# SBUF tiles at chosen distances from one another, one r block in the attention's PSUM banks, and the last down projection in token rows

## The chip, the cores and the metric

One core of one Trainium2 chip runs the whole program. The metric is the device time of one execution in microseconds (us), smaller is better. The kernel before takes 1268.01 us, the median of 3 runs (1267.92 to 1268.65).

## The reference

A decoder trunk of two layers over 256 tokens of width 1024, in float32. Each layer is a half-step SwiGLU (hidden width 2816), a mixer of two parallel branches (a three-branch sparse attention with 8 heads and a chunked gated linear attention, called GLA, with 4 heads), and a second half-step SwiGLU; a final RMS norm ends it.

```python
def swiglu(x, w_gate, w_up, w_down):
    return (jax.nn.silu(x @ w_gate) * (x @ w_up)) @ w_down
...
    for l in range(DEPTH):
        x = x + 0.5 * swiglu(rmsnorm(x, ffn1_norm[l]), ffn1_w_gate[l], ffn1_w_up[l], ffn1_w_down[l])
        h = rmsnorm(x, mix_norm[l])
        proj = h @ w_in[l]
        q_a, kv_a, g_a, q_b, k_b, v_b, a_lr, r_b, g_merge = jnp.split(proj, offsets, axis=-1)
...
        o_b = o_b.reshape(B, S, GLA_HEADS * GLA_DV) * jax.nn.silu(r_b)
        gm = jax.nn.sigmoid(g_merge).reshape(B, S, 2, D)
        y = gm[:, :, 0] * (o_a @ w_branch_nsa[l]) + gm[:, :, 1] * (o_b @ w_branch_gla[l])
        x = x + y @ w_out[l]
        x = x + 0.5 * swiglu(rmsnorm(x, ffn2_norm[l]), ffn2_w_gate[l], ffn2_w_up[l], ffn2_w_down[l])
    return rmsnorm(x, final_norm)
```

## The kernel before

**Numbers in two parts.** Every large product is made of three: a float32 value is kept as a rounded high part and a low part, and high times high, high times low and low times high are summed in PSUM. `mm3` writes these as three matmuls. `mm2` writes them as two: the high weight against the activation's high and low part side by side (512 passing columns), then the low weight against the high part alone (256). A matmul has a standing operand (128 x 128, loaded into TensorE by a weight load) and a passing operand (streamed through it).

**Which operand stands.** In `ffn`, `T_pair`, the `wo` products and the down projections (tiles `ff`, `mm` of 256 columns, `wo`, `dn`) the weights stand and the activations pass, so the result has features on partitions. In `block` and the merge (`mm` of 512 columns, `mg`) the activations stand and a row of 512 weights passes, so the result has tokens on partitions. The last output feature block (j = 7) of `dn` and `wo` uses `mm3` with 256 passing columns.

**Weights.** `Weights` holds one list of chunks in the order of use. SP loads a chunk into one of 3 `raw` tiles, ScalarE rounds it into `wh` (`cast`, line 76) and VectorE subtracts it into `wl` (line 86), half a chunk at a time; `prep` is called between the matmuls of the chunk ahead, and `take` hands a chunk out. Each of `wh` and `wl` has 3 tiles.

**Memory.** Tiles lie in SBUF in the order in which the pools are opened: constants (with the `xs` tiles that hold the activation's two parts), small ones, `t4` (15 tiles of 4 KB a partition: the hidden values `h`, `oa`, `ob`, `y` and more), `t2` (9 of 2 KB), `raw`, `wh` and `wl`. In the built program, taken modulo 512 bytes, the `xs` tiles start at 128, the `t4`, `t2`, `raw`, `wh` and `wl` tiles at 480. All slices that a large matmul reads start at a multiple of 512 bytes from their tile's start (but for `vg`). In this text the distance of a matmul is the start of its standing slice less the start of its passing slice, modulo 512 bytes: 352 where weights stand against `xs` (`ff`, `mm` of 256 columns), 0 where they stand against `t4` tiles (`dn`, `wo`), 160 where `xs` stands and weights pass (`mm` of 512 columns), 0 where `oa` and `ob` stand and weights pass (`mg`).

**PSUM.** Two banks have the tag `mm`, six the tag `sd`, each set used in turn. In the mixer the main stream of `block` uses the two `mm` banks: two blocks for v, two for r (the gate's input, evacuated by `r_evac`: a tanh on ScalarE, then a multiply-add on VectorE, line 541), four for the merge gates (`gm`). `slot` drives the side work (attention, then GLA) from generators between the matmuls, in the `sd` banks. A block's first matmul waits until its bank has been read out.

**The end.** After the last down projection (`next_gain is None`), `add_half` adds each feature block to x, a square on ScalarE and a sum over feature blocks give the norm, `final_x` transposes x times the final gain into token rows (tile `fin`), one matmul of ones gives each token's sum, GpSimd raises it to -1/2, and ScalarE and VectorE scale four 128 x 512 tiles, which SP writes out with four transfers.

Of the kernel before, what the change touches and what calls it, by code (L numbers as in the profile page):

```python
# [15 lines left out]
P = 128  # L16
# [19 lines left out]

class Weights:
# [10 lines left out]
    def load(self, n):  # L48
        while self.n_load < min(n, len(self.chunks)):
            ap, rows, cols = self.chunks[self.n_load]  # L50
# [11 lines left out]
    def cast(self):  # L62
# [13 lines left out]
        self.nc.scalar.activation(wh[:, s], self.raw[c][:, s], AF.Copy)  # L76
# [3 lines left out]
    def prep(self):  # L80
# [5 lines left out]
        self.nc.vector.tensor_sub(wl[:, s], self.raw[c][:, s], wh[:, s].bitcast(F32))  # L86
# [5 lines left out]
    def take(self):  # L92
        c = self.n_take
        self.n_take += 1
        while self.n_prep < (c, 1):
            self.prep()
        _, rows, cols = self.chunks[c]
        wh, wl = self.split.pop(c)
        return tuple(x[:, : rows * cols].rearrange("p (r c) -> p r c", c=cols) for x in (wh, wl))


class Trunk:
# [63 lines left out]
    def square(self, j, own=False):  # L166
# [5 lines left out]
        elif own:  # L172
            self.own = sq
        else:
            self.nc.vector.tensor_add(self.acc, self.acc, sq)
# [52 lines left out]
    def final_x(self, j):  # L228

        if j == 0:  # L230
            self.fin = [[self.bank(f"fin{t}{e}") for e in range(2)] for t in range(2)]
        xg = self.xg.pop(j)
        for tt in range(2):
            self.nc.tensor.transpose(self.fin[tt][j // 4][:, j % 4 * P : j % 4 * P + P], xg[:, tt * P : tt * P + P], self.ident)


    def ffn(self, l, f, next_gain, hook=None):
# [14 lines left out]
        def gate2(u):  # L252
            nc.vector.tensor_mul(u[:, 0:T], u[:, 0:T], self.rbc)
# [64 lines left out]
        while lows:  # L318
            low()
        for j in range(NK):  # L320
            b = self.bank(f"dn{self.uid()}", "mm")
            for half in range(2):
# [7 lines left out]
                if next_gain is None and half == 0 and j > 0:  # L330
                    self.final_x(j - 1)
                    if j == NK - 1:
                        self.st = self.bank("stl")
                        self.sums(self.acc, True, False)
            self.add_half(j, b)
            if next_gain is None:
                self.square(j, own=j == NK - 1)
                xg = self.t2(f"xg{j}")[:, 0:T]
                nc.vector.tensor_scalar(xg, self.x[j], self.final[:, j : j + 1], None, op0=OP.mult)
                self.xg[j] = xg  # L340
            else:
                self.post_x(j, next_gain[:, j : j + 1])
# [10 lines left out]
    def add_half(self, j, b):  # L353
        for s in (slice(0, T), slice(T, 2 * T))[: 2 if j < NK - 1 else 1]:
            self.nc.vector.scalar_tensor_tensor(self.x[j], b[:, s], 0.5, self.x[j], op0=OP.mult, op1=OP.add)  # L355


    def mixer(self, l, next_gain):
# [152 lines left out]
        def block(evac):  # L511

            bs = [self.bank(f"mm{self.uid()}", "mm") for _ in range(2)]
# [32 lines left out]
        for n in range(2):  # L546
            block(r_evac(n))
# [514 lines left out]
    def go(self):  # L1062
# [3 lines left out]
        with ExitStack() as st:  # L1066
# [33 lines left out]
            self.xg = {}  # L1100
            self.w1 = {}
            sm = cp.tile([P, 80], F32, name="sm")
# [217 lines left out]
```

## Time and profile before

| what | value |
|---|---|
| median of 3 runs | 1268.01 us (1267.92 to 1268.65) |
| the profiled execution: its own time, and its span | 1268.17 us, 1266.4 us |
| busy share of TensorE (PE), VectorE, ScalarE, GpSimd | 99%, 72%, 56%, 4% |
| mean granted clock of TensorE | 0.998 of full |
| moved from and to HBM | 225.12 MB, 2.63 MB; 180 GB/s over the span |

The span runs from the first to the last instruction that the trace shows; the execution's own time is 1.8 us longer. A PE row's length is a modelled pipeline time and longer than the pace: the matmuls overlap, so the pace is read from the starts of rows that follow one another.

### The profile page before, as it was taken

How to read it: one execution, taken by the hardware profiler on the slowest of the kernel's cores; microseconds unless marked ns; L12 is line 12 of the kernel's file. 1: busy time of each engine (PE TensorE's matmuls, PEld its weight loads, DVE VectorE, ACT ScalarE, POOL GpSimd, SP SyncE). 2: the span in 40 equal slices, each digit the busy share in tenths (PEclk: the TensorE clock that was granted, in tenths of full speed). 3: DMA queues.
4: the chain of work that ended last, by engine and by line, in shares of the span. 5: the costliest groups of instructions: out<-in, count | busy, mean ns of one | idle time of the engine just before them, and what ended most of it. 6: DMA issues, size and time to landing. Idle time of an engine off the chain costs nothing.

```text
span 1266.4 us, 18985 instructions
## 1 busy us (share of the span) xinstructions
PE 1251.6 (99%) x7396; PEld 1076.0 (85%) x7396; DVE 913.9 (72%) x1690; ACT 711.8 (56%) x1265; POOL 50.5 (4%) x60
## 2 busy tenths in 40 slices
PE   9999999999999999999999999999999999999997
PEld 7888889987778888888888888999777788888886
DVE  6888766774755778886578886567656668888753
ACT  5666545566644556655456664456675445566542
POOL 2001101000010000000010000010000100000000
PEclk9999999999999999999999999999999999999999
DMA  7576767334534445545665546573344354555451
GB/s 272 193 230 211 255 201 264 132 124 137 178 118 144 181 168 205 187 154 198 209 224 208 179 150 205 173 283 135 111 156 164 103 199 148 184 200 185 165 190 59
DMA packets 41001, 227.43 MB, mean 180 GB/s; under 512 B 6949, under 2 KB 8109, under 8 KB 21328
## 3 DMA queue, kind: packets, MB, share of 16 engines
q1 hardware_dynamic: 34352, 213.27, 48.7%
q0 software_dynamic: 5840, 11.87, 2.8%
q8 instruction: 58, 0.95, 0.3%
q10 hardware_dynamic: 720, 1.09, 0.3%
q14 instruction: 31, 0.25, 0.1%
HBM read 225.12 MB, written 2.63 MB: 180 GB/s over the span
## 4 chain that ended last, share of the span: by engine, by line
PE 80%; issue 15%; DVE 2%; ACT 2%; DMA 1%; POOL 0%; POOLq 0%; DVEq 0%; ACTq 0%
PE ff L129 19%; PE ff L130 10%; PE dn L129 9%; PE mm L122 7%; PE mm L123 6%; PE mm L124 6%; PE dn L130 4%; PE wo L129 2%; PE mg L122 2%; PE mg L124 2%; PE mg L123 2%; PE O L150 2%; PE o L150 1%; PE s L150 1%; PE wo L130 1%
## 5 line engine op out<-in xcount | busy, mean ns | idle before, releaser
L76 ACT ACTIVATE wh<-raw 128x1024 fp32r<-128x1024 f32 (+3 forms) x445 | 423.4, 967 | 183.6 <-issue 112.3
L86 DVE TENSOR_TENSOR wl<-raw,wh 128x1024 fp32r<-128x1024 f32 (+3 forms) x445 | 491.3, 1119 | 44.0 <-ACT wh L76 43.7
L129 PE MATMUL ff<-xs,wh 128*128 128x512 f32 x1408 | 489.9, 392 | 0.4 <-DVE xs L162 0.4
L130 PE MATMUL ff<-xs,wl 128*128 128x256 f32 x1408 | 393.9, 280 | 0.7 <-DVE wl L1144 0.5
L129 PEld LDWEIGHTS ff<-xs,wh 128*128 128x128 f32 x1408 | 264.4, 188 | 59.2 <-ACT wh L1143 0.8
L130 PEld LDWEIGHTS ff<-xs,wl 128*128 128x128 f32 x1408 | 264.3, 188 | 1.7 <-DVE wl L1144 1.1
L129 PE MATMUL dn<-h,wh 128*128 128x512 f32 x616 | 218.3, 399 | 0.0
L130 PE MATMUL dn<-h,wl 128*128 128x256 f32 x616 | 173.0, 281 | 0.0
L129 PEld LDWEIGHTS dn<-h,wh 128*128 128x128 f32 x616 | 115.7, 188 | 28.3
L139 DVE TENSOR_TENSOR u<-ff,u 128x256 f32<-128x256 f32 x176 | 74.7, 425 | 60.9 <-ACT u L138 60.9
L130 PEld LDWEIGHTS dn<-h,wl 128*128 128x128 f32 x616 | 116.4, 189 | 0.0
L122 PE MATMUL mm<-wh,xs 128*128 128x512 f32 x256 | 106.2, 415 | 2.5 <-DVE rt L541 2.5
L123 PE MATMUL mm<-wl,xs 128*128 128x512 f32 x256 | 101.5, 396 | 0.0
L124 PE MATMUL mm<-wh,xs 128*128 128x512 f32 x256 | 100.9, 394 | 0.0
L249 ACT ACTIVATE u<-u 128x256 f32<-128x256 f32 x88 | 36.8, 419 | 90.8 <-DVE u L248 90.8
L261 ACT ACTIVATE h<-u 128x256 fp32r<-128x256 f32 x88 | 36.8, 418 | 83.9 <-DVE u L260 83.9
L122 PE MATMUL mm<-xs,wh 128*128 128x256 f32 x256 | 73.8, 288 | 0.0
L124 PE MATMUL mm<-xs,wl 128*128 128x256 f32 x256 | 71.7, 280 | 0.0
L123 PE MATMUL mm<-xs,wh 128*128 128x256 f32 x256 | 71.6, 280 | 0.0
L138 ACT ACTIVATE u<-ff 128x256 f32<-128x256 f32 x176 | 65.6, 373 | 9.8 <-PE ff L130 5.4
L355 DVE SCALAR_TENSOR_TENSOR xs<-dn,xs 128x256 f32<-128x256 f32 x60 | 25.5, 424 | 56.0 <-PE dn L130 38.5
L122 PEld LDWEIGHTS mm<-wh,xs 128*128 128x128 f32 x256 | 48.1, 188 | 19.3 <-issue 4.7
(244 smaller groups left out, 1618.1 us busy)
## 6 DMA issues: line engine op xcount, KB each, us to landing
raw<-in_gu SPq DMA_DIRECT2D x85, 1024.0 KB, 4.9
raw<-in_wd SPq DMA_DIRECT2D x64, 704.0 KB, 4.1
raw<-in_wr SPq DMA_DIRECT2D x32, 1024.0 KB, 4.8
raw<-in_wt SPq DMA_DIRECT2D x16, 1024.0 KB, 5.1
raw<-in_wb SPq DMA_DIRECT2D x12, 1024.0 KB, 4.8
w<-in_w POOLq DMA_DIRECT2D x16, 512.0 KB, 8.6
raw<-in_wo SPq DMA_DIRECT2D x8, 1024.0 KB, 4.9
raw<-in_vg SPq DMA_DIRECT2D x4, 592.0 KB, 3.7
```

The source lines that it names most:

```text
L76: self.nc.scalar.activation(wh[:, s], self.raw[c][:, s], AF.Copy)
L86: self.nc.vector.tensor_sub(wl[:, s], self.raw[c][:, s], wh[:, s].bitcast(F32))
L122: mm(out, lh, rh, start=first, stop=False, skip_group_check=True)
L123: mm(out, lh, rl, start=False, stop=False, skip_group_check=True)
L124: mm(out, ll, rh, start=False, stop=last, skip_group_check=True)
L129: mm(b, lh, x[2], start=first, stop=False, skip_group_check=True)
L130: mm(b[:, 0:T], ll, x[0], start=False, stop=last, skip_group_check=True)
L138: self.nc.scalar.activation(o, b[:, T : 2 * T], AF.Copy)
L139: self.nc.vector.tensor_add(o, b[:, 0:T], o)
L150: self.nc.tensor.matmul(out, l, r, start=first, stop=last, skip_group_check=True)
L249: nc.scalar.activation(g, g, AF.Silu)
L261: nc.scalar.activation(hs[i][0], h, AF.Copy)
```

## The change

The weight tiles get 2176 columns in place of 2048, and chunks whose weights pass (`vg`, `wr`, `wb` and the new `wl`) are written 40 columns (160 bytes) into them, by the fourth entry of a chunk. Two unused tiles (`gap0`, 512 bytes, before `t4`; `gap1`, 352 bytes, before `wh`) move the pools, the `sm` tile loses 8 columns, and the memory set aside for GpSimd's transfer descriptors is halved to 8192 bytes a partition. In the built program, modulo 512 bytes, `xs` stays at 128, `t4`, `t2` and `raw` start at 128 and `wh` and `wl` at 480, so a chunk written 160 bytes on starts at 128. The distance is then 352 for every product with standing weights (`ff`, `mm` of 256 columns, `dn`, `wo`) and 0 for every one with passing weights (`mm` of 512 columns, `mg`, the new last `dn`).

The second r block takes its two banks from the `sd` set. The last down projection (`last_down`) lets weights pass and `h` stand: x enters the four token-row banks first by 16 float32 matmuls with the identity, then 11 chunks of four weight rows follow, the last three for one token half and then for the other; the factor 0.5 moves into `gate2`. The squares come from PSUM with a running sum, the gain is a row that GpSimd loads by broadcast, and each token half is written out by two transfers, on ScalarE's and SP's queues. The old path (`final_x`, the sums, four transfers at the end) is gone.

```diff
+SHIFT = 40
...
-        _, rows, cols = self.chunks[c]
+        _, rows, cols, off = self.chunks[c]
         if part == 0:
             self.split[c] = tuple(
-                self.pools["w"].tile([P, 2048], F32R, name=f"w{x}{c}", tag=f"w{x}") for x in "hl"
+                self.pools["w"].tile([P, 2176], F32R, name=f"w{x}{c}", tag=f"w{x}") for x in "hl"
             )
         wh, wl = self.split[c]
         cut = (rows + 1) // 2 * cols
         s = slice(0, cut) if part == 0 else slice(cut, rows * cols)
-        self.nc.scalar.activation(wh[:, s], self.raw[c][:, s], AF.Copy)
+        self.nc.scalar.activation(wh[:, s.start + off : s.stop + off], self.raw[c][:, s], AF.Copy)
         self.cast_done.append((c, part, s))
...
-        self.nc.vector.tensor_sub(wl[:, s], self.raw[c][:, s], wh[:, s].bitcast(F32))
+        off = self.chunks[c][3]
+        o = slice(s.start + off, s.stop + off)
+        self.nc.vector.tensor_sub(wl[:, o], self.raw[c][:, s], wh[:, o].bitcast(F32))
...
         def gate2(u):
-            nc.vector.tensor_mul(u[:, 0:T], u[:, 0:T], self.rbc)
+            if next_gain is None:
+                nc.vector.scalar_tensor_tensor(u[:, 0:T], u[:, 0:T], 0.5, self.rbc, op0=OP.mult, op1=OP.mult)
+            else:
+                nc.vector.tensor_mul(u[:, 0:T], u[:, 0:T], self.rbc)
...
         while lows:
             low()
+        if next_gain is None:
+            self.last_down(hs)
+            return
         for j in range(NK):
             b = self.bank(f"dn{self.uid()}", "mm")
             for half in range(2):
...
-                if next_gain is None and half == 0 and j > 0:
-                    self.final_x(j - 1)
-                    if j == NK - 1:
-                        self.st = self.bank("stl")
-                        self.sums(self.acc, True, False)
             self.add_half(j, b)
-            if next_gain is None:
-                self.square(j, own=j == NK - 1)
-                xg = self.t2(f"xg{j}")[:, 0:T]
-                nc.vector.tensor_scalar(xg, self.x[j], self.final[:, j : j + 1], None, op0=OP.mult)
-                self.xg[j] = xg
-            else:
-                self.post_x(j, next_gain[:, j : j + 1])
+            self.post_x(j, next_gain[:, j : j + 1])
...
+    def last_down(self, hs):
+        nc, W = self.nc, self.W
+        bs = [[self.bank(f"dn{e}{tt}", "sd" if e else "mm") for tt in range(2)] for e in range(2)]
+        pre = [self.small([P, 2], f"pre{tt}", 1) for tt in range(2)]
+        xg = [[self.t2(f"xg{e}{tt}") for tt in range(2)] for e in range(2)]
+        def residual(e):
+            for tt in range(2):
+                for q in range(4):
+                    self.mm(bs[e][tt][:, q * P : q * P + P], self.x[4 * e + q][:, tt * P : tt * P + P], self.ident, q == 0, False)
+        def products(c, tt, wh, wl):
+            for r in range(4):
+                e, k = divmod(4 * c + r, NFF)
+                s = slice(tt * P, tt * P + P)
+                self.mm3(bs[e][tt], hs[k][0][:, s], hs[k][1][:, s], wh[:, r], wl[:, r], False, k == NFF - 1)
+        def gained(e, tt):
+            sq = self.t2(f"fsq{e}{tt}")
+            nc.scalar.activation(sq, bs[e][tt], AF.Square, accum_out=pre[tt][:, e : e + 1])
+            nc.vector.tensor_mul(xg[e][tt], bs[e][tt], self.fin[:, e * 512 : e * 512 + 512])
+        def first(tt):
+            gained(0, tt)
+            nc.vector.tensor_scalar(pre[tt][:, 0:1], pre[tt][:, 0:1], 1.0 / D, EPS, op0=OP.mult, op1=OP.add)
+        def finish(tt):
+            gained(1, tt)
+            ms = self.small([P, 1], "fms")
+            nc.vector.tensor_scalar(ms, pre[tt][:, 1:2], 1.0 / D, pre[tt][:, 0:1], op0=OP.mult, op1=OP.add)
+            rs = self.small([P, 1], "frs")
+            nc.gpsimd.tensor_tensor(rs, ms, self.mhalf[:, 0:1], op=OP.pow)
+            for e in range(2):
+                o = xg[e][tt]
+                if e == 0:
+                    nc.scalar.activation(o, o, AF.Copy, scale=rs)
+                    nc.scalar.dma_start(self.out[tt, :, 0:512], o)
+                else:
+                    nc.vector.tensor_scalar(o, o, rs, None, op0=OP.mult)
+                    nc.sync.dma_start(self.out[tt, :, 512:1024], o)
+        residual(0)
+        for c in range(8):
+            if c == 5:
+                residual(1)
+            wh, wl = W.take()
+            for tt in range(2):
+                products(c, tt, wh, wl)
+                W.prep()
+            if c in (3, 4):
+                W.prep()
+            if c == 5:
+                for tt in range(2):
+                    first(tt)
+        ws = [W.take() for _ in range(3)]
+        for tt in range(2):
+            for x in range(3):
+                products(8 + x, tt, *ws[x])
+            finish(tt)
...
-        def block(evac):
-            bs = [self.bank(f"mm{self.uid()}", "mm") for _ in range(2)]
+        def block(evac, tag="mm"):
+            bs = [self.bank(f"mm{self.uid()}", tag) for _ in range(2)]
...
-            block(r_evac(n))
+            block(r_evac(n), ("mm", "sd")[n])
...
+            gap = pool("gap", 1)
+            gap.tile([P, 128], F32, name="gap0")
             self.pt4 = pool("t4", 15)
             self.pt2 = pool("t2", 9)
-            pools = dict(raw=pool("raw", N_RAW), w=pool("w", N_SPLIT))
+            pools = dict(raw=pool("raw", N_RAW))
+            pool("gap2", 1).tile([P, 88], F32, name="gap1")
+            pools["w"] = pool("w", N_SPLIT)
...
-                        chunks.append((a["gu"][l, f, i], 16, P))
+                        chunks.append((a["gu"][l, f, i], 16, P, 0))
+                    if (l, f) == (L - 1, 1):
+                        for i in range(11):
+                            chunks.append((a["wl"][i], 4, 512, SHIFT))
+                        return
                     for i in range(16):
-                        chunks.append((a["wd"][l, f, i], 11, P))
+                        chunks.append((a["wd"][2 * l + f, i], 11, P, 0))
                 ffn_chunks(0)
                 wt = [(a["wt"][l, i], 16, P) for i in range(8)]
-                vg = [(a["vg"][l, i], 4, 296) for i in range(2)]
-                chunks += wt[:1] + vg + wt[1:] + [(a["wr"][l, i], 4, 512) for i in range(16)]
-                chunks += [(a["wb"][l, i], 4, 512) for i in range(6)]
-                chunks += [(a["wo"][l, i], 16, P) for i in range(4)]
+                wide = lambda n, k, c: [(a[n][l, i], 4, c, SHIFT) for i in range(k)]
+                wt = [w + (0,) for w in wt]
+                chunks += wt[:1] + wide("vg", 2, 296) + wt[1:] + wide("wr", 16, 512) + wide("wb", 6, 512)
+                chunks += [(a["wo"][l, i], 16, P, 0) for i in range(4)]
...
+                def gain_row(i):
+                    if i == 11:
+                        self.fin = self.t4("fin")
+                        nc.gpsimd.dma_start(self.fin, a["fin"].broadcast_to([P, D]))
...
-    nc = _bacc.Bacc("TRN2", target_bir_lowering=False, num_devices=1)
+    nc = _bacc.Bacc("TRN2", target_bir_lowering=False, num_devices=1, dynamic_dma_scratch_size=8192)
```

The moves that the order of instructions shows, on the engines that wait or are waited for:

TensorE, first mixer, from the last matmuls of the second r block to the first of the merge gates (`mm` is the PSUM bank written, then passing and standing operand), before:

```order
1875 L122 MATMUL mm_3311<-wh_3250,xs_97 128x512
1876 L123 MATMUL mm_3311<-wl_3251,xs_97 128x512
1877 L124 MATMUL mm_3311<-wh_3250,xs_97 128x512
1878 L122 MATMUL mm_3406<-wh_3301,xs_90 128x512 [waits DVE_49]
1879 L123 MATMUL mm_3406<-wl_3302,xs_90 128x512
1880 L124 MATMUL mm_3406<-wh_3301,xs_90 128x512
```

The same place in the changed kernel:

```order
1875 L129 MATMUL mm_3319<-wh_3258,xs_105 128x512
1876 L130 MATMUL mm_3319<-wl_3259,xs_105 128x512
1877 L131 MATMUL mm_3319<-wh_3258,xs_105 128x512
1878 L129 MATMUL mm_3414<-wh_3309,xs_98 128x512 [waits Activation_49]
1879 L130 MATMUL mm_3414<-wl_3310,xs_98 128x512 [waits DVE_49]
1880 L131 MATMUL mm_3414<-wh_3309,xs_98 128x512
```

The first gate matmul waited for VectorE before, which is the read-out of the r block's bank; in the changed kernel it waits for ScalarE and the next for VectorE, for the two parts of its weights.

TensorE, the start of the last down projection in the changed kernel (before, `dn` matmuls with standing weights followed the `ff` matmuls directly):

```order
6601 L137 MATMUL ff_11353<-xs_105,wl_11239 128x256
6602 L157 MATMUL dn_11406<-cst,xs 128x128 [waits DMAHW0_49]
6603 L157 MATMUL dn_11406<-cst,xs 128x128 x3
6604 L157 MATMUL dn_11407<-cst,xs 128x128 x4
6605 L129 MATMUL dn_11406<-wh_11291,h_704_10293 128x512 [waits Activation_49]
6606 L130 MATMUL dn_11406<-wl_11292,h_704_10293 128x512 [waits DVE_49]
6607 L131 MATMUL dn_11406<-wh_11291,h_704_10293 128x512
```

Eight float32 matmuls of x with the identity stand ahead of the first product, and the products come in threes of 512 columns.

VectorE, the end of the program, before (`xs` is x, `st` the sums) and then changed:

```order
1671 L355 SCALAR_TENSOR_TENSOR xs<-dn_11815,xs 128x256 [waits PE_49]
1672 L355 SCALAR_TENSOR_TENSOR xs<-dn_11815,xs 128x256 [waits DVE_49]
1673 L175 TENSOR_TENSOR sq_11459<-sq_11459,sq_11873 128x256 [waits Activation_49]
1674 L339 TENSOR_SCALAR xg_11876<-xs,sm 128x256 [waits DVE_49]
1675 L355 SCALAR_TENSOR_TENSOR xs<-dn_11878,xs 128x256 [waits PE_49]
1676 L339 TENSOR_SCALAR xg_11953<-xs,sm 128x256 [waits DVE_49]
1677 L192 TENSOR_SCALAR ms_11957<-stl 128x2 [waits PE_49]
1678 L1231 TENSOR_SCALAR out_11966<-fin_11495,rs_11959 128x512 [waits PE_49,Pool_49]
1679 L1231 TENSOR_SCALAR out_11972<-fin_11497,rs_11959 128x512 [waits PE_49]
```

```order
1642 L371 TENSOR_TENSOR xg_11414<-dn_11408,fin 128x512 [waits Activation_49]
1643 L380 TENSOR_SCALAR fms_11734<-pre_776_11410 128x1 [waits DVE_49]
1644 L389 TENSOR_SCALAR xg_11414<-xg_11414,frs_11736 128x512 [waits Pool_49]
1645 L371 TENSOR_TENSOR xg_11415<-dn_11409,fin 128x512 [waits Activation_49]
1646 L380 TENSOR_SCALAR fms_11781<-pre_777_11411 128x1
1647 L389 TENSOR_SCALAR xg_11415<-xg_11415,frs_11783 128x512 [waits Pool_49]
```

The additions to x, the gained copy and the read of the sums are replaced, for each token half, by one product with the gain row, one small step and one scaling; the product waits for ScalarE, whose square reads the same bank.

## Rows read from the trace of the kernel before

**Rows 1.** The page's first part: busy us, share of the span, instructions.

```profile
PE 1251.6 (99%) x7396; PEld 1076.0 (85%) x7396; DVE 913.9 (72%) x1690; ACT 711.8 (56%) x1265; POOL 50.5 (4%) x60
```

**Rows 2.** Busy us (count) of PE, PEld, DVE, ACT, POOL, PEclk, DMA share, GB/s.

```profile
311.79:325.55 13.76, 13.76 (x61) 11.09 (x60) 9.52 (x13) 13.70 (x20) 0.00 (x0) 1.00 0.38 127
...
460.00:570.00 110.00, 110.00 (x636) 96.87 (x636) 93.67 (x165) 68.11 (x123) 0.00 (x0) 1.00 0.52 179
...
1193.50:1257.54 64.04, 64.04 (x394) 57.05 (x392) 35.79 (x60) 24.26 (x37) 0.00 (x0) 1.00 0.42 136
```

**Rows 3.** Timeline of PE in `ff`, 58 pairs apart: start, us, what.

```profile
499.81 0.39 PE L129 MATMUL ff<-xs,wh 128*128 128x512 f32 x1
...
519.91 0.39 PE L129 MATMUL ff<-xs,wh 128*128 128x512 f32 x1
```

**Rows 4.** Timeline of PE in `dn` of the first layer's second half-step, 43 pairs apart.

```profile
594.77 0.28 PE L130 MATMUL dn<-h,wl 128*128 128x256 f32 x1
...
609.96 0.28 PE L130 MATMUL dn<-h,wl 128*128 128x256 f32 x1
```

**Rows 5.** Timeline of PE, 66 matmuls of `dn` (j = 7), then 47 of `mm`.

```profile
188.61 0.28 PE L122 MATMUL dn<-h,wh 128*128 128x256 f32 x1
...
196.52 0.28 PE L122 MATMUL mm<-xs,wh 128*128 128x256 f32 x1
...
202.04 0.28 PE L124 MATMUL mm<-xs,wl 128*128 128x256 f32 x1
```

**Rows 6.** Timeline of PE in the r blocks: 59 matmuls from first to second.

```profile
311.80 0.39 PE L122 MATMUL mm<-wh,xs 128*128 128x512 f32 x1
...
325.56 0.39 PE L124 MATMUL mm<-wh,xs 128*128 128x512 f32 x1
```

**Rows 7.** Timeline of PE in the merge: 71 matmuls from first to second.

```profile
389.96 0.40 PE L122 MATMUL mg<-wh,oa 128*128 128x512 f32 x1
...
406.10 0.39 PE L124 MATMUL mg<-wh,ob 128*128 128x512 f32 x1
```

**Rows 8.** Groups by line and form on PE: count | busy us, mean ns | idle before.

```profile
L129 PE MATMUL dn<-h,wh 128*128 128x512 f32 x616 | 218.3, 399 | 0.0
L122 PE MATMUL mm<-wh,xs 128*128 128x512 f32 x256 | 106.2, 415 | 2.5 <-DVE rt L541 2.5
L129 PE MATMUL wo<-y,wh 128*128 128x512 f32 x112 | 40.5, 404 | 0.4 <-DVE y L577 0.4
```

**Rows 9.** Timeline of PE, first matmul of the merge gates, in the first mixer.

```profile
327.18 0.50 PE L122 MATMUL mm<-wh,xs 128*128 128x512 f32 x1 [1.23 <-DVE rt L541]
```

**Rows 10.** The waits of PE: who for whom, us in total, times, longest.

```profile
PE mm L122 <- DVE rt L541: 2.5, 2, 1.2
```

**Rows 11.** Timeline of VectorE around it: the second half of two weight chunks.

```profile
321.70 1.20 DVE L86 TENSOR_TENSOR wl<-raw,wh 128x1024 fp32r<-128x1024 f32 x1
...
328.33 1.22 DVE L86 TENSOR_TENSOR wl<-raw,wh 128x1024 fp32r<-128x1024 f32 x1
```

**Rows 12.** Timeline of PE: four float32 matmuls of 128 columns (eight records), and what follows.

```profile
337.30 1.05 PE L150 MATMUL ab<-qr,ga 128*128 128x128 f32 x8
338.11 0.48 PE L122 MATMUL mm<-wh,xs 128*128 128x512 f32 x1
```

**Rows 13.** Timeline of all engines from the last matmul of `dn` on.

```profile
1257.41 0.28 PE L124 MATMUL dn<-h,wl 128*128 128x256 f32 x1
1257.73 0.42 DVE L355 SCALAR_TENSOR_TENSOR xs<-dn,xs 128x256 f32<-128x256 f32 x1 [6.46 <-PE dn L124]
...
1258.72 0.61 PE L150 MATMUL stl<-ones,sq 128*128 128x1 f32 x4 [1.02 <-ACT sq L169]
...
1260.32 1.41 DVE L1231 TENSOR_SCALAR out<-fin,rs 128x512 f32<-128x512 f32 x2 [0.80 <-POOL rs L194]
1261.04 1.80 SPq L1232 DMA_DIRECT2D out<-out  x4
```

**Rows 14.** Timeline of ScalarE: the reading of a running sum after a square.

```profile
353.35 0.19 ACT L849 ACTIVATION_READ_ACCUMULATOR on<-o 128x1 f32 x1
```

More of the change, by code (lines that the diff above doesn't have):

```diff
@@ L49, in load @@
         while self.n_load < min(n, len(self.chunks)):
-            ap, rows, cols = self.chunks[self.n_load]
+            ap, rows, cols, _ = self.chunks[self.n_load]
             t = self.pools["raw"].tile([P, 2048], F32, name=f"raw{self.n_load}", tag="raw")
@@ L96, in take @@
             self.prep()
-        _, rows, cols = self.chunks[c]
+        _, rows, cols, off = self.chunks[c]
         wh, wl = self.split.pop(c)
-        return tuple(x[:, : rows * cols].rearrange("p (r c) -> p r c", c=cols) for x in (wh, wl))
+        return tuple(x[:, off : off + rows * cols].rearrange("p (r c) -> p r c", c=cols) for x in (wh, wl))
 class Trunk:
@@ L164, in split_x, with square @@
         )
-    def square(self, j, own=False):
+    def square(self, j):
         sq = self.psq.tile([P, T], F32, name=f"sq{self.uid()}", tag="sq" if j else "acc")
@@ L226, in lead_pair @@
             self.rstd_col()
[L228 to L234, printed above, removed]
     def ffn(self, l, f, next_gain, hook=None):
@@ L1099, in go @@
             self.xh, self.xl = [x[0] for x in self.xx], [x[1] for x in self.xx]
-            self.xg = {}
             self.w1 = {}
-            sm = cp.tile([P, 80], F32, name="sm")
+            sm = cp.tile([P, 72], F32, name="sm")
             first = pools["raw"].tile([P, 2048], F32, name="raw0", tag="raw")
-            view = lambda t, p: t.rearrange("p (n k c) -> p n k c", n=2, k=NK)[:, :, 2 * p : 2 * p + 2, :]
+            view = lambda t, p: t[:, 0:2048].rearrange("p (n k c) -> p n k c", n=2, k=NK)[:, :, 2 * p : 2 * p + 2, :]
             for p in range(4):
@@ L1138, in go @@
             nc.vector.memset(self.mhalf, -0.5)
-            w0 = W.split[0] = tuple(pools["w"].tile([P, 2048], F32R, name=f"w{x}0", tag=f"w{x}") for x in "hl")
+            w0 = W.split[0] = tuple(pools["w"].tile([P, 2176], F32R, name=f"w{x}0", tag=f"w{x}") for x in "hl")
             for p in range(4):
@@ L1144, in go @@
                 nc.vector.tensor_sub(view(w0[1], p), view(first, p), view(w0[0], p).bitcast(F32))
-            w1 = W.split[1] = tuple(pools["w"].tile([P, 2048], F32R, name=f"w{x}1", tag=f"w{x}") for x in "hl")
+            w1 = W.split[1] = tuple(pools["w"].tile([P, 2176], F32R, name=f"w{x}1", tag=f"w{x}") for x in "hl")
             for s in (slice(0, 512), slice(512, 1024)):
@@ L1218, in go @@
                 self.mixer(l, gain(l, 2))
-                self.ffn(l, 1, gain(l + 1, 0) if l + 1 < L else None)
-            self.sums(self.own, False, True)
-            self.rstd_col()
-            self.final_x(NK - 1)
-            for tt in range(2):
-                for e in range(2):
-                    o = self.t2(f"out{tt}{e}")
-                    b = self.fin[tt][e]
-                    if e == 0:
-                        nc.scalar.activation(o, b, AF.Copy, scale=self.rs[:, tt : tt + 1])
-                    else:
-                        nc.vector.tensor_scalar(o, b, self.rs[:, tt : tt + 1], None, op0=OP.mult)
-                    nc.sync.dma_start(self.out[tt, :, e * 512 : e * 512 + 512], o)
+                self.ffn(l, 1, gain(l + 1, 0) if l + 1 < L else None, gain_row if l + 1 == L else None)
 def _bucket(n):
@@ L1270, in _layout @@
         [pj(v[n][l]) for l in range(L) for n in ("ffn1_norm", "mix_norm", "ffn2_norm")]
-        + [pj(v["final_norm"])] + [pj(v["gla_out_norm"][l]) for l in range(L)]
+        + [pj(v["gla_out_norm"][l]) for l in range(L)]
         + [pj(v["gla_a_b"][l]) for l in range(L)], axis=1))
@@ L1285, in _layout @@
     a["gu"] = c(np.stack(gu).reshape(L, 2, NFF, P, 2048))
-    a["wd"] = c(np.stack(wd).reshape(L, 2, 16, P, 11 * P))
+    a["wd"] = c(np.stack(wd))
+    a["fin"] = c(v["final_norm"][None])
     wt, vg, wr, wb, wo = [], [], [], [], []
```

11 lines of the change are left out of this document (6 added, 5 removed).

## The prediction

> **What bounds the kernel now.** I read the page's busy times first: TensorE is busy for 99% of the span [rows 1], so the time is the sum of its matmuls' slots plus an end in which it has nothing to do. The table of stretches shows that nothing slows its clock: the granted clock is 1.00, the level of 2.4 GHz, in each of them [rows 2]. At that level 512 passing columns last 213.3 ns and 256 last 106.7. The third view is the timeline of TensorE, read from start to start, and it shows that a matmul takes more than that, by an amount that depends on the stage. A pair of `mm2` (512 and 256 columns, 320 ns ideal) takes (519.91 - 499.81) / 58 = 346.6 ns in `ff` [rows 3] and (609.96 - 594.77) / 43 = 353.3 ns in `dn` [rows 4]: the same two instructions, the same standing weights, another tile passing. A single matmul of 256 columns takes 7.91 / 66 = 119.8 ns in `dn` and 5.52 / 47 = 117.4 ns in `mm` [rows 5]. A matmul of 512 columns with weights passing takes 13.76 / 59 = 233.2 ns in the r blocks [rows 6] and 16.14 / 71 = 227.3 ns in the merge [rows 7]. The four paces sort by the distance that the address arithmetic of the kernel gives: 352 is quicker than 0 where weights stand, 0 quicker than 160 where they pass. A pace is steady within a class whose starts differ only by multiples of 512 bytes, which is why I read the distance modulo 512.
>
> **The change, part by part.**
>
> *Standing weights move from distance 0 to 352.* This concerns `dn` in the three half-steps that keep it, and `wo`. After the change both sides lie modulo 512 exactly as in `ff` (128 and 480), so its pace is the nearest row. There are 616 pairs of `dn` in four half-steps [rows 8], 462 in the three: 462 x 6.7 ns = 3.1 us. The 66 singles of each of the three: 198 x 2.4 ns = 0.5 us. `wo` has 112 pairs [rows 8] and 48 singles at the same distance as `dn`: 0.75 + 0.1 us. Together 4.4 us. The lower bound is nothing, the upper this sum.
>
> *Passing weights move from distance 160 to 0.* This concerns the `mm` matmuls of 512 columns: 256 for each of three lines [rows 8], 768. The nearest row is the merge, whose distance is 0 before and after: 768 x (233.2 - 227.3) ns = 4.5 us. It is less certain than the first part, since both operands then lie at 128 and in the merge of before both lay at 480; no row shows 128 against 128. A quarter of these matmuls (the v blocks) is woven with attention, where TensorE may reach a wait sooner; that can cost 1.1 us at most, I take off 0.4. So 4.1 us, bounds 0 and 4.5.
>
> A rule of the Trainium skill speaks against both parts: "SBUF — State Buffer", section "Who interferes with whom", gives TensorE two independent read ports, one for the passing operand and one for weight loads, and says that it never waits on anyone. By that rule distance is worth nothing and the sum below would be 4.8 us in place of 13.3; the paces of [rows 3 to 7] differ all the same between identical instructions, so I follow the rows and keep the rule's result as a rival.
>
> *`ff` and the 256-column `mm`* keep their distance of 352 and get nothing.
>
> *The second r block in `sd` banks.* Before, the first gate matmul waits for the read-out of the r block's bank: TensorE starts a matmul at 325.56 and the next at 327.18, 1.39 us over a slot of 0.233 [rows 6, 9]; it is VectorE's line 541 both times that it occurs, 1.2 us of idle each [rows 10]. With the r block elsewhere, the gate block's banks are those of the first r block, long read out. What is late next is the weights. The second half of the gate block's first chunk is subtracted from 321.70 to 322.90 [rows 11] and is ready. The next chunk's second half ends at 329.55; TensorE, starting at 325.8, needs that chunk after 24 matmuls of 0.227, at 331.3. That leaves 1.7 us, so the wait goes: 2 x 1.4 = 2.8 us, bounds 0 (it returns there) and 2.8. ScalarE is the engine to watch, busy for 13.70 of 13.76 us ahead of it [rows 2].
>
> *The last down projection.* Before, the stage lasts 64.04 us from its first to its last matmul's slot [rows 2]. Now it has 11 chunks x 4 rows x 2 token halves x 3 = 264 matmuls of 512 columns. At the merge's pace they last 60.0 us. The 16 identity matmuls are like the four `ab` ones, 0.81 us for four (337.30 to 338.11, and the matmul behind them is recorded at 0.48 us where others show 0.39 [rows 6, 12]): 3.2 us, and some 0.2 for the changes of form. The transposes and token sums inside the stage go. So 63.5, a gain of 0.5 us, bounds -1.0 (264 x 233.2 ns) and 0.8. Casts and subtractions of 1024 columns stay two a chunk of 24 x 0.227 = 5.5 us; VectorE is busy for 36 of 64 us there [rows 2], and that cover is enough.
>
> *The end.* Before, the chain from the last matmul's start runs 1257.41 to 1261.04, when the first output transfer is issued; four issues take 1.80 us on SP; the span ends at 1266.4, 3.56 later [rows 13]. Now the chain swaps an addition (0.42), a square of its size and the token sums (0.61) for a square of 512 columns with the reading of its running sum (0.19 [rows 14]) and a product of 512 columns (0.70, half of the 1.41 [rows 13]), which waits for that square. It also starts 0.1 later behind a matmul of twice the columns. That comes out even, within 0.3 us. SP issues one transfer behind it, not four: 3/4 of 1.80 = 1.35 us. The first token half is scaled and written under the second's 36 matmuls, 8.2 us. I take 1.5 us, bounds 1.0 and 2.1 (fewer transfers share the landing).
>
> *At nothing:* the factor in `gate2` (one VectorE instruction for another of the same size), the gain row's load (GpSimd, one half-step early) and the smaller descriptor memory (no row shows GpSimd's queue near the path). Casts and subtractions now read and write at distances of their own; in `ff` VectorE is busy for 93.67 of 110 us [rows 2], which covers 0.41 us for each half chunk.
>
> Sum: 4.4 + 4.1 + 2.8 + 0.5 + 1.5 = 13.3 us. The profiled execution took 1268.17 us, 0.16 over the median of the runs; from the median, 1268.0 - 13.3 = **1254.7 us**.
>
> **The rivals.**
>
> *A. Only standing weights gain.* If the pace hangs on where the passing tile itself lies, or 128 against 128 is as poor as 160, then `mm` stays at 233.2 and the last projection runs at it too: 4.1 + 1.6 us lost, 1260.4. For it: no row has this pair of places. Against: [rows 6, 7] are the same instruction and differ with the distance.
>
> *B. The wait comes back elsewhere.* TensorE reaches the chunk or the GLA matmuls earlier and ScalarE, full in [rows 2], or VectorE ends last: 2.8 us lost, 1257.5.
>
> *C. Distance does nothing.* The change then doesn't do what its layout says: 8.5 us lost, 1263.2, left with the r block and the end. This is what the skill's rule gives. Against it stands [rows 3, 4].
>
> *D. VectorE becomes the bound: slower.* The subtraction reads `raw` and `wh`, at one place modulo 512 before and 352 apart after. If two inputs of VectorE mind that as TensorE's do, it grows from 1.2 us [rows 11]. In `ff` it is covered up to 1.6 us; beyond that each 0.1 us costs 88 chunks x 2 x 0.1 = 17.6 us. At 1.7 us the time is 1272, and from there on it is slower. No row shows VectorE minding addresses.
>
> **How the numbers follow.** A measurement of this kernel tells a change from none at about 0.2%, 2.5 us. Chances: forecast 0.66 (its own range 1251.5 to 1257.5, from the bounds of the end, the v blocks and the last projection), A 0.13, B 0.09, C 0.07, D 0.05. The range takes in A and B and some of C's side: 1250.5 to 1262. All but D and what I have not thought of are faster by over 2.5 us: 0.92; within it 0.03; slower 0.05.
>
> **What would show it.** In the profile after: `dn` and `wo` pairs at 346 to 347 ns from start to start (else C), `mm` of 512 columns and the last `dn` at 227 to 228 (else A); `ff` unchanged; no wait of an `mm` matmul for `rt`, and no new one for weights or GLA (else B); the last projection at 63 to 64 us, and from its last matmul to the span's end 7 to 8 us in place of 9.0; subtractions of the same length (else D). The prediction is wrong if the pace of `mm` doesn't follow the distance, or if VectorE's instructions lengthen.

## The result, and the profile after

The changed kernel takes **1254.88 us**, the median of 4 runs (1254.61 to 1254.97); the kernel before takes 1267.97 in the runs beside it (1267.55 to 1268.65). The ratio is 0.9896, with an interval of 0.9879 to 0.9913. The profiled execution took 1254.97 us, 1253.2 of them span. It is faster by 13.1 us, or 1.0%. The granted clock is 0.999 in it and 0.998 before, the level of 2.4 GHz, and 0.997 to 1.000 in every run below, so no reading below has to do with the clock. One run of experiment 3 took 2570.78 us, twice as long as the other three (1260.81 to 1261.02), and is left out of the comparisons.

The page's first part, against [rows 1]: TensorE is busy for 10.5 us less, and still for 99% of the span.

```profile
PE 1241.1 (99%) x7294; PEld 1070.1 (85%) x7294; DVE 903.6 (72%) x1658; ACT 710.4 (57%) x1255; POOL 50.8 (4%) x62
```

The paces, read from start to start in the timeline of TensorE (start, us, what). In order: 43 pairs of `dn` in the same half-step as [rows 4]; 66 single matmuls of `dn`, to the first one behind them, as in [rows 5]; 59 matmuls of the r blocks, as in [rows 6]; 71 of the merge, as in [rows 7].

```profile
570.38 0.39 PE L136 MATMUL dn<-h,wh 128*128 128x512 f32 x1
...
585.28 0.39 PE L136 MATMUL dn<-h,wh 128*128 128x512 f32 x1
...
187.69 0.28 PE L129 MATMUL dn<-h,wh 128*128 128x256 f32 x1
...
195.43 0.28 PE L129 MATMUL mm<-xs,wh 128*128 128x256 f32 x1
...
313.02 0.39 PE L129 MATMUL mm<-wh,xs 128*128 128x512 f32 x1
...
326.40 0.39 PE L131 MATMUL mm<-wh,xs 128*128 128x512 f32 x1
...
385.73 0.39 PE L129 MATMUL mg<-wh,oa 128*128 128x512 f32 x1
...
401.82 0.39 PE L131 MATMUL mg<-wh,ob 128*128 128x512 f32 x1
```

The pair of `dn` is at 14.90 / 43 = 346.5 ns (353.3 before), the single at 7.74 / 66 = 117.3 (119.8), the r blocks at 13.38 / 59 = 226.8 (233.2), the merge at 16.09 / 71 = 226.6 (227.3). The 59 matmuls from 313.02 on run through the place where TensorE stood still in [rows 9]. The waits of TensorE (who for whom, us in total, times, longest) have no `rt` any more; [rows 10] had 2.5 us. These are all above 0.5 us. The one for `xs` is at the program's first product; it was 0.39 us before, and it varies from 0.2 to 1.4 us among runs whose instructions there are the same:

```profile
PE wb L157 <- DVE mhalf L1198: 1.5, 1, 1.5
PE ff L136 <- DVE xs L169: 1.3, 1, 1.3
PE yt L623 <- DVE ym L676: 0.9, 2, 0.4
```

VectorE's subtraction (group by form: count | busy, mean ns | idle before) is as long as [rows 11] show it, although in the chunks whose weights stand its two inputs now lie 352 bytes apart (where weights pass, the shift of 160 puts `wh` at 128, where `raw` lies). The 167 of them under way in `ff` have a mean of 1218 ns; before, 164 had 1219:

```profile
L93 DVE TENSOR_TENSOR wl<-raw,wh 128x1024 fp32r<-128x1024 f32 x331 | 400.7, 1218 | 42.3 <-ACT wh L81 42.1
```

The end, from the last matmul on (timeline of all engines without weight loads), against [rows 13]:

```profile
1246.12 0.39 PE L131 MATMUL dn<-wh,h 128*128 128x512 f32 x1
1246.54 0.60 ACT L370 ACTIVATE fsq<-dn 128x512 f32<-128x512 f32 x1 [5.21 <-PE dn L131]
1247.04 0.19 ACT L370 ACTIVATION_READ_ACCUMULATOR fsq<-dn 128x1 f32 x1
1247.26 0.69 DVE L371 TENSOR_TENSOR xg<-dn,fin 128x512 f32<-128x512 f32 x1 [6.17 <-ACT fsq L370]
...
1248.15 0.55 POOL L382 TENSOR_TENSOR frs<-fms,mhalf 128x1 f32<-128x1 f32 x1 [7.58 <-DVE fms L380]
1248.74 0.72 ACT L386 ACTIVATE xg<-xg,frs 128x512 f32<-128x512 f32 x1 [1.51 <-POOL frs L382]
1248.74 0.49 DVE L389 TENSOR_SCALAR xg<-xg,frs 128x512 f32<-128x512 f32 x1 [0.67 <-POOL frs L382]
1249.26 0.34 SPq L390 DMA_DIRECT2D out<-xg  x1
1249.49 0.35 ACTq L387 DMA_DIRECT2D out<-xg  x1
```

The chain from the last matmul's start to the last issue is 3.37 us (3.63 before, to the first issue); then one issue of 0.35 us follows where four took 1.80; the span ends 3.3 us after it (3.56). GpSimd's raising to -1/2 stands in both chains, before for two columns:

```profile
1259.60 0.69 POOL L194 TENSOR_TENSOR rs<-ms,mhalf 128x2 f32<-128x2 f32 x1 [181.08 <-DVE ms L192]
```

Up to its start the chain takes 2.03 us (2.19 before), from there to the scaling 0.59 (0.72), and from the scaling to the issue 0.75 (0.72).

Where the 13.1 us come from is seen best by stage. The table has the time from the first matmul of a stage to the first of the next, worked out from the starts in each trace; for the mixer, the merge and `wo` of one layer (the two layers agree within 0.05 us unless both are given), for `dn` of one of the three half-steps.

| us | before | after | e3 no shift | e4 old distances | e5 r block alone | e6 r block back | e7 all zero |
|---|---|---|---|---|---|---|---|
| `dn` (x3) | 62.32 | 61.13 | 61.13 | 62.32 | 62.32 | 61.13 | 61.30, 62.33, 62.33 |
| mixer up to the merge (x2) | 193.45 | 190.30 | 191.75 | 191.73 | 191.71 | 192.51 | 190.29 |
| merge (x2) | 34.00 | 33.96 | 34.82 | 34.00 | 34.00 | 33.96 | 33.96 |
| `wo` (x2) | 24.32 | 23.94 | 23.94 | 24.32 | 24.32 | 23.93 | 24.32, 24.01 |
| last projection, first to last start | 63.91 | 63.25 | 64.94 | 63.23 | 63.91 | 63.25 | 63.25 |
| last start to span's end | 8.98 | 7.06 | 7.07 | 7.06 | 8.99 | 7.06 | 7.05 |

The `ff` stages are 122.93 or 122.94 us in every column. What lies ahead of the first `dn` (start and first `ff`) varies from 133.9 to 134.6 us among these runs; the changed kernel has 134.31, the kernel before 134.20.

### The profile page after: what moved, and what is told of

It reads as the page before. It is cut to its first block, busy times and chain, and to the rows that moved or that the text cites. A ratio compares the mean times of both kernels' runs of the same rounds, so it can differ in the third digit from the quotient of the medians.

```text
span 1253.2 us, 18722 instructions
## 1 busy us (share of the span) xinstructions
PE 1241.1 (99%) x7294; PEld 1070.1 (85%) x7294; DVE 903.6 (72%) x1658; ACT 710.4 (57%) x1255; POOL 50.8 (4%) x62
## 4 chain that ended last, share of the span: by engine, by line
PE 96%; issue 1%; DVE 1%; ACT 1%; DMA 1%; POOL 0%; POOLq 0%; ACTq 0%; DVEq 0%
PE ff L136 25%; PE ff L137 13%; PE dn L136 8%; PE mm L129 7%; PE mm L131 7%; PE mm L130 7%; PE dn L137 4%; PE dn L129 2%; PE dn L130 2%; PE dn L131 2%; PE wo L136 2%; PE mg L131 2%; PE mg L129 2%; PE mg L130 2%; PE O L157 2%; PE o L157 1%
## 5 line engine op out<-in xcount | busy, mean ns | idle before, releaser
L136 PE MATMUL dn<-h,wh 128*128 128x512 f32 x462 | 160.3, 392 | 0.0
L137 PE MATMUL dn<-h,wl 128*128 128x256 f32 x462 | 129.1, 280 | 0.0
L136 PEld LDWEIGHTS dn<-h,wh 128*128 128x128 f32 x462 | 86.7, 188 | 19.2
L137 PEld LDWEIGHTS dn<-h,wl 128*128 128x128 f32 x462 | 86.7, 188 | 0.0
L129 PEld LDWEIGHTS mm<-wh,xs 128*128 128x128 f32 x256 | 48.1, 188 | 14.3 <-issue 4.7
L131 PEld LDWEIGHTS mm<-wh,xs 128*128 128x128 f32 x256 | 48.0, 188 | 10.7
```

Source lines behind the costliest of these rows:

```text
L129: mm(out, lh, rh, start=first, stop=False, skip_group_check=True)
L131: mm(out, ll, rh, start=False, stop=last, skip_group_check=True)
L136: mm(b, lh, x[2], start=first, stop=False, skip_group_check=True)
L137: mm(b[:, 0:T], ll, x[0], start=False, stop=last, skip_group_check=True)
```

## The experiments

Each is the changed kernel with the edit shown, except the fifth, which is the kernel before. The theory was that TensorE's pace hangs on the distance modulo 512 bytes between standing and passing starts, and that the r block's wait and the end come on top. The first rival was that distance does nothing.

**1, 2. Sweeps of the distance.** Chunks of weights (all but the first two and those of `wt` and `wo`) begin at scattered places of their tiles; in the second sweep `xs` and everything behind it up to `raw` moves by 96 bytes as well.

```diff
+def step(n, by):
+    return 4 * (n * by % 32) if n > 1 else 0
-   chunks.append((a["gu"][l, f, i], 16, P, 0))
+   chunks.append((a["gu"][l, f, i], 16, P, step(len(chunks), 11)))
...
-   wide = lambda n, k, c: [(a[n][l, i], 4, c, SHIFT) for i in range(k)]
+   wide = lambda n, k, c: [(a[n][l, i], 4, c, step(2 + 32 * l + i + 16 * (n == "wb"), 7)) for i in range(k)]
```

And in the second sweep alone:

```diff
-   pool("gap2", 1).tile([P, 88], F32, name="gap1")
+   pool("gap2", 1).tile([P, 64], F32, name="gap1")
...
+   cp.tile([P, 24], F32, name="pad")
```

> Every weight chunk but the first two of the program (and the four without shift in the code) begins 4*k floats further into its tile, k from 0 to 31 in a scattered order, so the distance from standing to passing start runs over 512 bytes in steps of 16, for standing weights (ff, dn) and for passing weights (mm, mg, last dn). By the theory that the distance modulo 512 alone sets the pace: undisturbed passing chunks at distance 0 run at 226.7 ns a matmul and at 160 at 233.5 ns, standing pairs at 352 at 346.6 ns and at 0 at 353.3 ns, whichever chunk it is, with other distances between or beyond; the whole then lies between 1254 and 1275 us. By the rival that the two tiles do not meet in memory at all: one pace for all distances, 226.7 and 346.6 ns, total 1254.9 us.

> The same scattered shifts, and xs and all tiles up to the raw ones lie 96 bytes further on, the weight tiles where they were. If the distance decides, the curve of pace over distance is that of the sweep before within 1 ns, so as a curve over the shift it is moved by 96 bytes. If the place of the weights themselves decides (their start modulo 512 or 64), the pace over the shift stays as it was. If neither matters, all are 226.7 and 346.6 ns again.

They took 1264.75 and 1268.07 us, one run each. Mean ns of an undisturbed `ff` pair by distance (512 + 256 columns; steps of 400 ns or more, which are stalls, left out; each figure from 31 to 60 pairs), in the second sweep by the distance as it then is:

```
distance          0     16     32     48     64     80     96    112    128    144    160    176    192    208    224    240
sweep 1       346.9  347.2  347.0  346.8  353.1  353.4  347.2  353.2  350.9  349.2  351.5  350.6  349.2  349.2  347.0  347.9
 same + 256   346.9  347.3  347.0  346.8  353.1  353.4  347.7  353.3  350.7  349.2  351.5  350.5  349.4  349.2  347.0  347.9
sweep 2       346.9  347.2  347.0  346.8  353.2  353.4  347.1  353.3  350.9  349.1  352.4  350.9  349.4  349.2  347.1  346.8
```

The weights in the second sweep are where they were, `xs` is not, and the curve stays put over the distance, within 0.3 ns but for 160 and 240, where it is 1 ns: so, but for the exceptions below, the pace follows the distance and not the weights' own place. It repeats after 256 bytes, not 512. No distance has a quicker steady pace than those that the change had chosen, 346.7 for a pair at 352 and 226.7 for a passing row at 0.

The second sweep from 256 on agrees with the row shown within 0.3 ns at all distances but 256 and 288, where the means are 348.8 and 349.9 in place of 346.9 and 347.0. At 256 it is the first two chunks of the program, with long stretches of 350, 361 and 349 ns in turn. At 288 it is one chunk: its pairs take 346 and 361 ns in turn, while those of the three other chunks at 32 and 288 take 347. The two rows are 12 pairs of that chunk apart, 353.3 ns a pair:

```profile
46.81 0.40 PE L140 MATMUL ff<-xs,wh 128*128 128x512 f32 x1
...
51.05 0.40 PE L140 MATMUL ff<-xs,wh 128*128 128x512 f32 x1
```

So one distance can have more than one pace. `wo`, whose weights the sweeps leave in place, stands at 256 in the second sweep and takes 24.32 and 24.31 us there, as long as at 0 before. Passing weights have a curve too, with the same exception. Beyond the first eight rows behind a break, the first sweep has 236.8 ns at 16, 233.5 at 64, 231.1 at 176, and 228.9 at 192 in the merge and the last projection; the second has 236.7, 233.5, 231.1 and 228.8. But the two chunks of the blocks at 448 (192 modulo 256) run at 233.3 in the first sweep, and the chunk of the last projection at 336 runs at 230.9 in the first sweep and at 233.3 in the second.

One more figure did not fit: standing weights at distance 0 ran at 346.9 ns here, and at 353.3 in [rows 4]. Experiment 7 takes that up.

**3. No shift of the passing weights.**

```diff
-SHIFT = 40
+SHIFT = 0
```

> SHIFT = 0: all passing weights go from distance 0 to distance 160, the standing ones stay at 352. 768 matmuls of the mixer's blocks, 288 of the merge and 264 of the last down projection. By the paces that the prediction used, 227.3 against 233.2 ns: 1320 x 5.9 = 7.8 us more, 1262.7 us. By the paces now measured (229.0 to 233.2 in the blocks, 226.7 to 233.5 elsewhere): 768 x 4.2 + 552 x 6.8 = 7.0 us more, 1261.9 us. If distance does nothing: 1254.9 us.

Measured: 1261.00 us, ratio to the kernel before 0.9944 (0.9924 to 0.9964). So 6.1 us are lost: by the table 2 x 1.45 in the mixer, 2 x 0.86 in the merge, 1.69 in the last projection, less 0.3 at the start. The two rows are the first and the last of 59 steps in the r blocks, at 233.4 ns:

```profile
313.19 0.39 PE L129 MATMUL mm<-wh,xs 128*128 128x512 f32 x1
...
326.96 0.39 PE L131 MATMUL mm<-wh,xs 128*128 128x512 f32 x1
```

The rival of no effect is refuted here by one constant, which moves the time by 6.1 us. But the mixer gains only 2.9 us where the prediction had 4.1. The timelines show why. In the changed kernel the undisturbed pace is 226.7, and the mean over the 702 clean products of the blocks is 229.0: behind each break in the stream (a step of the attention or GLA work) some eight to ten matmuls run unevenly. This is the stream of the merge in the changed kernel behind the transposes `yt`, whose pace ahead of them is 226.7:

```profile
402.41 0.47 PE L129 MATMUL mg<-wh,oa 128*128 128x512 f32 x1
402.72 0.39 PE L130 MATMUL mg<-wl,oa 128*128 128x512 f32 x1
402.95 0.39 PE L131 MATMUL mg<-wh,oa 128*128 128x512 f32 x1
403.18 0.40 PE L129 MATMUL mg<-wh,oa 128*128 128x512 f32 x1
403.41 0.39 PE L130 MATMUL mg<-wl,oa 128*128 128x512 f32 x1
403.64 0.40 PE L131 MATMUL mg<-wh,oa 128*128 128x512 f32 x1
403.87 0.39 PE L129 MATMUL mg<-wh,oa 128*128 128x512 f32 x1
404.10 0.39 PE L130 MATMUL mg<-wl,oa 128*128 128x512 f32 x1
404.33 0.39 PE L131 MATMUL mg<-wh,oa 128*128 128x512 f32 x1
```

From 402.72 to 404.33 are seven steps of 230 ns (in the trace's nanoseconds 224, 231, 236, 228, 233, 230, 227). At distance 160 the same seven steps take 233 ns, and so do all others: 702 clean products, mean 233.3. So 66 breaks in the blocks cost 702 x (229.02 - 226.67) ns = 1.65 us behind them at distance 0, 25 ns each, and nothing at 160.

**4. The old distances with the new banks and the new last projection.**

```diff
-SHIFT = 40
+SHIFT = 0
...
-gap.tile([P, 128], F32, name="gap0")
+gap.tile([P, 216], F32, name="gap0")
...
-pool("gap2", 1).tile([P, 88], F32, name="gap1")
```

> The distances of the kernel before (dn and wo 0, mm 160, merge and last down projection 0, ff 352) with the r block and the last down projection of the changed kernel. The standing part gave 3.57 + 0.76 us between the two profiles, the blocks 768 x 4.2 = 3.2 us: 1254.9 + 7.5 = 1262.4 us. If distance does nothing and all came from the banks and the last down projection: 1254.9 us. The prediction's sum would make it 1254.9 + 8.5 = 1263.4 us.

Measured: 1261.91 us, 0.9951 (0.9936 to 0.9966). All distances together are worth 7.0 us beside the other two parts: 3 x 1.19 for `dn`, 2 x 0.38 for `wo`, 2 x 1.43 for the mixer, 0.1 for the merge, less 0.4 at the start.

**5. The r block alone, in the kernel before.**

```diff
-def block(evac):
-    bs = [self.bank(f"mm{self.uid()}", "mm") for _ in range(2)]
+def block(evac, tag="mm"):
+    bs = [self.bank(f"mm{self.uid()}", tag) for _ in range(2)]
...
-    block(r_evac(n))
+    block(r_evac(n), ("mm", "sd")[n])
```

> The kernel before with one edit: the second r block in the attention banks. Prediction: the 1.4 us wait at its first product goes in both layers, 2.8 us less, 1265.2 us. The two profiles with old distances and new banks show 193.44 - 191.75 = 1.7 us a layer less, so 3.4 us, 1264.6 us. By the rival that the wait comes back at a later product of the block: 1268.0 us.

Measured: 1264.18 us, 0.9974 (0.9964 to 0.9984), so 3.5 us, 2 x 1.74 by the table. The prediction's 1.39 us a layer is the wait for the first bank. With it go the slower start behind it and a smaller wait for the second token half's bank: in the trace of before the steps from start to start after 327.18 show 335, and twelve products on 348 and 336 ns, where 233 is the pace; 1.39 + 0.10 + 0.12 + 0.10 = 1.71 us.

**6. The r block back, in the changed kernel.**

```diff
-    block(r_evac(n), ("mm", "sd")[n])
+    block(r_evac(n))
```

> The changed kernel with both r blocks in the same banks again. If the wait and the distances add up: 1254.9 + 3.4 = 1258.3 us (2.8 by the prediction's term, 1257.7 us). If the distances alone had hidden it (products come sooner, so the wait should rather grow, by the time the blocks are faster): at most 1258.8 us. If the wait is not there any more: 1254.9 us.

Measured: 1258.89 us, 0.9932 (0.9917 to 0.9947), 4.0 us above the changed kernel. The wait of TensorE is back, and it is longer than in [rows 10]:

```profile
PE mm L129 <- DVE rt L595: 3.2, 2, 1.6
```

The blocks run faster at distance 0. Counted from the mixer's first product, the last matmul of the r block starts 0.79 us sooner than before (128.25 in place of 129.04), but VectorE's read-out only 0.41 sooner (129.51 in place of 129.92), so the stand at the bank grows from 1.39 to 1.78 us. So of the mixer's 3.15 us a layer the banks alone give 1.74 and the distance alone 0.94 (193.45 to 192.51); together they give 0.47 more than that.

**7. Standing weights at distance 0 again, at another place.**

```diff
-   chunks.append((a["wd"][2 * l + f, i], 11, P, 0))
+   chunks.append((a["wd"][2 * l + f, i], 11, P, SHIFT))
...
-   chunks += [(a["wo"][l, i], 16, P, 0) for i in range(4)]
+   chunks += [(a["wo"][l, i], 16, P, SHIFT) for i in range(4)]
```

> The changed kernel with the weights of the first three down projections and of wo begun 40 floats further on, so that they stand at distance 0 from their passing tiles, as before, but both now start at 128 modulo 512 where they started at 480. If distance modulo 512 alone sets the pace: 353.3 ns a pair as before, 3.57 + 0.76 us more, 1259.2 us. If the sweeps are right, whose chunks at distance 0 ran at 346.8 ns a pair: 1254.9 to 1255.1 us, and it is the place or what stands around it that made the slow pace.

Measured: 1258.04 us, 0.9924 (0.9907 to 0.9940), 3.2 us above the changed kernel: neither answer. The timeline shows both at once. These are 43 pairs of `dn` in the first half-step, then 43 pairs in the second, with the same instructions, places and distance:

```profile
142.15 0.39 PE L136 MATMUL dn<-h,wh 128*128 128x512 f32 x1
...
157.06 0.39 PE L136 MATMUL dn<-h,wh 128*128 128x512 f32 x1
...
571.20 0.40 PE L136 MATMUL dn<-h,wh 128*128 128x512 f32 x1
...
586.39 0.40 PE L136 MATMUL dn<-h,wh 128*128 128x512 f32 x1
```

The first run at 14.91 / 43 = 346.7 ns a pair, the second at 15.19 / 43 = 353.3. From start to start the first repeat 230 and 117 ns, the second 236 + 113, 233 + 117 and 241 + 120, over whole half-steps. So at distance 0 TensorE has two steady rhythms, and stays in the one it falls into until something interrupts the stream: in the second layer's `wo` it changes from the slow to the quick one behind a step of 277 ns. The kernel before had both already. In its last half-step, where the transposes `fin` interrupt the stream between feature blocks, the pairs of two blocks run at 347.0 ns (42 of them) and those of the other five at 353.4 (106). The first two rows are 28 pairs apart (9.90 us), the last two 19 (6.58 us):

```profile
1194.55 0.40 PE L129 MATMUL dn<-h,wh 128*128 128x512 f32 x1
...
1204.45 0.40 PE L129 MATMUL dn<-h,wh 128*128 128x512 f32 x1
...
1214.07 0.39 PE L129 MATMUL dn<-h,wh 128*128 128x512 f32 x1
...
1220.65 0.39 PE L129 MATMUL dn<-h,wh 128*128 128x512 f32 x1
```

At distance 352 all 1855 pairs of `ff` and `dn` in the changed kernel that are not next to a stall have a mean of 346.7; the slow rhythm does not occur there.

**8. Fewer breaks.** Two steps of the side work after every four rows, in place of one after two rows and one after four.

```diff
-                        if r == 1:
-                            slot()
...
                     slot()
+                    slot()
```

> The changed kernel, the side work of the mixer's blocks let in once per four rows (two steps of it, one behind the other) and not once per two. If what keeps the blocks at 229.0 ns is the stretch behind each break in the stream (66 breaks, 25 ns each in the products behind them: 1.65 us in all, none at distance 160): a third to half of the breaks fall together, 0.5 to 1 us less, and the mean of the clean products falls to about 228 ns; total 1253.9 to 1254.4 us, if the two steps in a row don't wait for each other. If they do, a wait of 0.5 to 1.5 us shows at the second product in a row, and the total is 1255 to 1265 us. If the blocks are slower for another reason (the casts or the subtractions beside them), the mean stays at 229.0 ns.

Measured: 1259.56 us, 0.9937 (0.9922 to 0.9952), 4.7 us above the changed kernel. Interruptions of the blocks fall from 66 to 44, and the mean clean product from 229.0 to 228.4 ns, which is 0.4 us; 22 breaks fewer at 25 ns would give 0.55. But steps of the attention and of GLA now wait for one another (waits of TensorE; neither line stands in the list of the changed kernel):

```profile
PE O L157 <- ACT PT L1023: 4.7, 4, 1.5
...
PE ab L157 <- DVE ga L843: 0.5, 2, 0.3
```

No run beat the changed kernel.

## Why the prediction was right

The time came out 0.2 us from the forecast and each part gained by the mechanism forecast for it: paces that change with the distance, a wait that goes, a shorter end. That the sum is so close is luck: the passing weights fell 1.2 us short, the r block and the end gave 1.1 us more than forecast.

*Standing weights*, 4.4 forecast: 3 x 1.19 + 2 x 0.38 = 4.3 measured. The pace of `ff` carried over, as the step from [rows 3, 4] had it. What it had wrong is the reason, that a pace is steady within a class of distances modulo 512: distance 0 need not be slow, it has a slow rhythm beside the quick one (experiment 7, and the last half-step of the kernel before), and [rows 4] happened to lie in the slow one, as did the three half-steps and the `wo` that the change moved.

*Passing weights*, 4.1 forecast: 2.9 measured (experiment 3). This is the mis-sized term. It priced the blocks by the merge, whose stream is hardly interrupted, and took off 0.4 for waits. The steady gain is larger than forecast, 768 x (233.3 - 226.7) = 5.1 us, but 1.65 us are lost behind the breaks, and some 0.4 at them, since the 66 steps from start to start that the breaks lengthen take 22.1 us together at distance 0 and 22.2 at 160; the mixer's 256-column matmuls take 0.1 more. The doubt that 128 against 128 might be poor was unfounded: [rows 7] has 227.3 and the profile after 226.6.

*The r block*, 2.8 forecast: 3.5 alone in the kernel before (experiment 5), and 4.4 by the stages in the changed kernel (2 x 2.21, experiment 6, whose whole time is only 4.0 longer as its start is 0.4 shorter). The second bank's wait and the slow restarts were not counted, and the wait would have grown with the faster blocks.

*The last projection*, 0.5 forecast: 0.66. *The end*, 1.5 forecast: 1.92; one issue for four gave 1.45 where 1.35 was forecast, the chain is 0.26 shorter, inside the 0.3 that the prediction allowed (0.16 up to GpSimd's instruction, 0.13 from there to the scaling, which now needs GpSimd's result of one column and not of two), and the landing is 0.2 shorter.

*At nothing*: `ff` is unchanged, the subtraction of 1024 columns takes 1218 ns before and after (those of 768 and 640 columns together 1.81 us a chunk both times), and no wait of the mixer took the place of the one removed. Rival A falls with the 226.8 ns of the r blocks, rival B with the list of waits, rival D with the subtractions. Rival C, that distance does nothing, falls with experiment 3, where one constant moves the time by 6.1 us, and experiment 4, where it would have left 1254.9. It is what the Trainium skill's page "SBUF — State Buffer", section "Who interferes with whom", makes of the two read ports of TensorE; the traces here do not agree with it, since identical streams go from 226.7 to 233.4 ns. Of the pace itself the Trainium skill's page "TensorE: Matmul & The Clock Gate", section "Back-to-back issue gap", puts the gap of an isolated matmul at 2.4 GHz at some 2.5 ns more than its columns need; no run here shows such a matmul, and the best steady pace of 512 columns in any of these traces, with a weight load ahead of every matmul, is 13.4 ns more (226.7 against 213.3).

Not settled: what in the memory or in TensorE makes the pace depend on the distance, and what chooses the rhythm where a distance has more than one. In experiment 7 the first `dn` follows an `ff` pair of 230 + 117 ns and becomes quick, the other two follow one of 228 + 118 and become slow; in experiment 4, with both tiles at 480, all three are slow, one of them behind the pair of 230 + 117. That suggests that both the way in and the place have a part.

## What to carry to other kernels

Where TensorE is busy all the time, compare the start-to-start pace of identical matmuls in different stages: a difference of 2 or 3% can come from the distance between standing and passing addresses, and a sweep of it within one kernel (a different offset for each chunk) shows the good distances in one run, if each is met several times, since the same distance can run at two paces. Take a distance at which every entry ends in the quick rhythm, and price a stage that is interrupted by its own breaks, not by the pace of an undisturbed stage. A bank's wait grows when the work ahead of it gets faster, so two edits that look additive can be worth more together.

## What had not been expected

The pace repeats over the distance after 256 bytes. At distance 0 the same standing stream has two steady rhythms, 346.7 and 353.3 ns a pair, and keeps its own through a whole half-step of 154 pairs; both stand in the trace of the kernel before. A slow rhythm beside a quick one shows at 288 (32 modulo 256) too, in one chunk of the second sweep. Behind a break the passing stream needs some eight to ten matmuls to settle at distance 0, at a cost of about 25 ns, and none at distance 160, where it is always at the slow pace.
